# Small matmuls of attention and retention regrouped by array tile in a two-layer decoder step

## The chip, the core and the metric

The kernel runs on one core of a Trainium2 chip. The metric is device time in microseconds. Tensors lie in SBUF (128 partitions); TensorE multiplies a stationary operand (up to 128 rows by 128 columns, loaded first) with a moving one and adds into PSUM; VectorE (DVE), ScalarE (ACT) and GpSimd (POOL) do the rest, and SyncE (SP) issues most DMAs.

## The reference, cut to what matters

One inference step of a two-layer decoder: a prompt of 256 tokens and a sample group of 8 sequences with 8 new tokens each. Each layer projects x (2048 wide) to 13824 columns and runs three branches: A retention (4 heads), B pooling, C sliding-window attention (16 query heads on 4 key heads of 64). The parts that the change touches:

```python
def step(s, inp):                          # retention, one chunk
    qc, kc, vc = inp
    sc = jnp.einsum('bihd,bjhd->bhij', qc, kc) * dmask
    o = jnp.einsum('bhij,bjhv->bihv', sc, vc) + jnp.einsum('bihd,bhdv->bihv', qc, s) * q_decay
...
s = jnp.einsum('bnqkgd,bnskd->bnkgqs', qb, kb).astype(jnp.float32) * (HD_C ** -0.5)   # attention
...
s = jnp.where(valid[None, :, None, None], s + bias, jnp.finfo(jnp.float32).min)
m = jnp.maximum(jnp.max(s, -1, keepdims=True), sink)
p = jnp.exp(s - m)
p = p / (jnp.sum(p, -1, keepdims=True) + jnp.exp(sink - m))
o = jnp.einsum('bnkgqs,bnskd->bnqkgd', p.astype(vb.dtype), vb)
```

All inputs and results are fp32. A sample token attends to the last 128 cached keys of its sequence and to the new keys of that sequence up to itself; the prompt has no cache, so its first block of 128 queries sees only its own 128 keys and the second sees 256.

## The kernel before, in words

All 320 token columns (256 of the prompt, 64 of the samples) are the moving operand of the dense matmuls; the weights are stationary, in blocks of 128x128. Weights come in 596 chunks of 8 blocks. Each block is split into a high and a low fp32r part (`split_h` on ScalarE, `split_l` on VectorE, two chunks ahead; the load itself is issued six chunks ahead by SP into four buffers), and x likewise, so that each block makes three dense matmuls of 320 columns: h by xh, l by xh, h by xl (`block`, `block_low`). They fill PSUM tiles named `d`.

The small work is written as generators and put on lanes: `att` for attention, `ret0` and `ret1` for retention, and a list `misc`. After each chunk (24 dense matmuls) `pump` takes one step of each lane, unless the estimated backlog of ScalarE or VectorE is over a bound. A step's matmuls so stand in one block between two dense ones, in the order in which the steps are written; TensorE takes its instructions in that order. Small matmuls write PSUM tiles `p`, of which there are five, used in turn (`self.pp`); a new one waits until the one five allocations back has been read.

An fp32 matmul appears in the trace as two records (its weights in two parts); a transpose and an fp32r matmul as one. Where operands lie on 64 or 32 partitions, or the output on 64 or 32 partitions, a matmul uses only that part of the array's rows or columns: 64*128 means 64 rows and 128 columns.

`attention` runs once for each layer and pair of key heads (four times); `halves` are the two key heads' 64 partitions. Its items follow each other by one step each, with the stages score, first (bias and maximum), exponentials, scale, transpose:

- `block0(hf)`: scores of the first 128 prompt queries for one half, four fp32 matmuls on the 64 rows of this half; two items, two blocks. `values0` follows.
- `block1(hf, g)`: scores of the second 128 queries for two query heads, with 256 keys. q is split into high (on its half's rows) and low (on the other half's rows) in `qx`; `kx[:, hf]` holds the high part of k on both halves, `kx[r, 2]` the low part on the 64 rows of its half. Each head needs a matmul over 128 rows and a second over 64. The eight query heads of the pair make four items.
- `sample(c)`: four sequences at a time, two items. `make` multiplies with the new keys (64*128, 96 columns of `kT`), and for each sequence and half with the cache (`ck`, 64*32, 128 columns). `turned` transposes the weights; `values` has the cached values `cv` stationary and the weights moving, 32 columns for a sequence, half by half.

`retention` runs for each head and layer (eight times). In its fourth step it computes, for each c of 2, the sample outputs `po`: one full matmul (`c`, `smr`) and four that add the state's part on 32 output columns each (`a2` stationary, `s0` moving, 256 columns).

`block0`, `block1`, `sample` and the retention step are at lines 843 to 950 and 585 to 605; `mm`, `add_mm` and `tr` (L197, L201, L206) are the helpers under whose lines the matmuls stand in the profile, and `copy` (L176), `tt` (L183), `stt` (L187) those of ScalarE and VectorE.

Of the kernel before, what the change touches and what calls it, by code (L numbers as in the profile page):

```python
# [11 lines left out]
F32 = mybir.dt.float32  # L12
# [14 lines left out]
EXT = POOL_BUF + NP  # L27
HW = POOL_BUF + NT
EXTW = EXT + NB * HW
BUCKET_START = list(range(17)) + [19, 21, 24, 27, 31, 35, 40, 46, 52, 59, 67, 77, 87, 99, 113]  # L30
NEG = -3.0e38
ALPHA = (2.0 * DEPTH) ** 0.25
# [69 lines left out]
class Step:  # L102
# [197 lines left out]
    def setup(self):  # L300
        nc, io = self.nc, self.io
        self.ident = self.const("ident", [128, 128])
        make_identity(nc, self.ident[:])
        self.ident_r = self.cp.tile([128, 128], F32R, tag="ident_r", name="ident_r")
        nc.vector.tensor_copy(out=self.ident_r, in_=self.ident)
        self.ones = self.const("ones", [128, 128])
        nc.vector.memset(self.ones, 1.0)
        self.ones_r = self.cp.tile([128, 128], F32R, tag="ones_r", name="ones_r")
        nc.vector.memset(self.ones_r[:].bitcast(F32), 1.0)
        yield  # L310
        self.rot = self.const("rot", [128, 2, T], io["c_rot"], nc.sync)
# [12 lines left out]
        self.kdecS = self.const("kdecS", [128, HA, NT], io["c_kdecs"])  # L324
        self.cnt = self.const("cnt", [128, 4, 16], io["c_cnt"])
        self.pscale = self.const("pscale", [128, DEPTH, 8], io["pool_scale"])
        self.lng = self.const("lng", [128, DEPTH, 16], io["ln_g"])
        self.lnb = self.const("lnb", [128, DEPTH, 16], io["ln_b"])
        self.bmask = self.const("bmask", [128, 4, 80], io["c_bmask"])
        self.flip = self.const("flip", [128, 2], io["c_flip"])  # L330
        yield
        self.biasS = self.const("biasS", [128, 4, 160], io["bias_s"])


    def run(self):
# [210 lines left out]
    def retention(self, l, h, r):  # L546
# [48 lines left out]
        pS = self.p([128, 256])  # L595
        self.mm(pS, ktok[:, 0, :], vtok[:, 0, :])
        self.copy(s1, pS)
        for c in range(2):
            po = self.p([128, 256])
            self.mm(po, smr[:, c, :], vsT[:, c, :])  # L600
            for b in range(4):
                lo = (4 * c + b) * 32
                self.add_mm(po[32 * b:32 * b + 32, :], a2[:, 1, lo:lo + 32], s0[b // 2][:, b % 2, c, :])
# [123 lines left out]
    def done_kc(self, p, ps):  # L727
# [47 lines left out]
    def attention(self, l, p, a):  # L775
# [33 lines left out]
        self.copy(vn, pv[0:32, 2:4, :])  # L809
# [5 lines left out]
        kx = self.g([128, 3, 256], F32R, name="kx")  # L815
        pt0 = self.g([128, 2, 4, 128], name="pt0")
        for hf, r in enumerate(halves):
            self.copy(kx[r, hf, :], kT[r, 0:256])
# [8 lines left out]
        pt1 = []  # L827

        def soft(make, out):

# [3 lines left out]
                box["ps"] = make()  # L834

            def first():
                s, n, sink, nsink = out[0](box.pop("ps"))
                box["s"] = s
                box["f"] = self.softmax(s, n, sink, nsink)

# [1 line left out]

        def block0(hf):

            r = halves[hf]
# [7 lines left out]
            def biased(ps):  # L853
                s = self.m([128, 4, 128], name="sc")
                self.stt(s, ps, 0.125, bias[hf][:, :, 128:256], ALU.mult, ALU.add)
                return (s, 4, *sinks(hf, 0, 4))

            def turned(s):
# [12 lines left out]

        def block1(hf, g):

            r = halves[hf]
# [32 lines left out]

        def sample(c):

            sT = {}  # L910

            def make():
                ps = [self.p([128, 256]) for _ in range(2)]
                for hf, r in enumerate(halves):
                    self.mm(ps[hf][:, 160:256], qsf[r, c, :], kT[r, 192 + 32 * c:288 + 32 * c])
                for b in range(4):
                    o = slice(32 * b, 32 * b + 32)
                    for hf, r in enumerate(halves):
                        self.mm(ps[hf][o, 0:128], qsf[r, c, o], ck[r, 4 * c + b, :])
                return ps  # L920

            def biased(ps):
                s = self.m([128, 2, 160], name="sc")
                for hf in range(2):
                    bs = self.biasS[:, 2 * p + hf, :]
                    self.stt(s[:, hf, 0:128], ps[hf][:, 0:128], 0.125, bs[:, 0:128], ALU.mult, ALU.add)
                    self.stt(s[:, hf, 128:160], ps[hf][:, 224:256], 0.125, bs[:, 128:160], ALU.mult, ALU.add)
                ks = slice(2 * p, 2 * p + 2)
                return s, 2, self.sinkS[:, l, ks], self.nsinkS[:, l, ks]

            def turned(s):
                pt = self.p([128, 4, 128])
                for hf in range(2):
                    self.tr(pt[:, hf, :], s[:, hf, 0:128])
                    self.tr(pt[0:32, 2 + hf, :], s[:, hf, 128:160])
                t = sT[0] = self.m([128, 4, 128], name="sT")
                self.copy(t[:, 0:2, :], pt[:, 0:2, :])
                self.copy(t[0:32, 2:4, :], pt[0:32, 2:4, :])
# [11 lines left out]
            return soft(make, (biased, turned)) + [values]  # L950
# [204 lines left out]
def constants():  # L1155
# [24 lines left out]
    c = dict(c_bmask=bmask, c_flip=flip, c_rot=rot, c_dmask=dmask, c_qdec=qdec, c_kdec=kdec, c_kdecs=kdecs, c_masks=masks, c_cnt=cnt)  # L1180
    return {k: np.ascontiguousarray(v, dtype=f) for k, v in c.items()}


def bias_tables(rel):
# [6 lines left out]

    q, k = np.arange(128), np.arange(256)
    bp = table(128 + q[:, None] - k[None, :]).reshape(128, 256, 4, 4)
    b4, g, t = np.arange(128) // 32, np.arange(128) % 32 // 8, np.arange(128) % 8
    c = np.arange(160)
    new = t[:, None] - (c[None, :] - 128) % 8
    own = (c[None, :] - 128) // 8 == b4[:, None]
    dist = np.where(c[None, :] < 128, 128 + t[:, None] - c[None, :], np.where(own, new, -1))
    bs = table(dist).reshape(128, 160, 4, 4)[np.arange(128), :, :, g]
    return dict(bias_p=bp.transpose(2, 0, 3, 1), bias_s=bs.transpose(0, 2, 1))  # L1200


# [91 lines left out]
```

## Time and profile before

| | |
|---|---|
| median of 3 runs | 2295.2 us |
| lowest and highest run | 2294.62, 4468.45 us |
| profiled execution: its own time | 2294.67 us |
| profiled execution: span | 2292.8 us |
| mean granted TensorE clock | 0.995 of full speed |
| TensorE / VectorE / ScalarE / GpSimd busy | 99% / 53% / 41% / 4% |
| DMA, mean over the span | 155 GB/s |

The highest run stands apart from the other two by a factor of two; the median and the profiled execution agree with the lowest. The span is what the profiler saw between the first and the last instruction; 1.9 us of the execution lie outside it. The page gives each engine's busy time first, then the span in 40 slices, then groups of instructions with their count, their total and mean time and the idle time in front of them. Matmuls are pipelined: their recorded durations overlap, so the distance between starts, as the timeline shows it, is what one of them costs.

### The profile page before, as it was taken

How to read it: one execution, taken by the hardware profiler on the slowest of the kernel's cores; microseconds unless marked ns; L12 is line 12 of the kernel's file. 1: busy time of each engine (PE TensorE's matmuls, PEld its weight loads, DVE VectorE, ACT ScalarE, POOL GpSimd, SP SyncE). 2: the span in 40 equal slices, each digit the busy share in tenths (PEclk: the TensorE clock that was granted, in tenths of full speed). 3: DMA queues.
4: the chain of work that ended last, by engine and by line, in shares of the span. 5: the costliest groups of instructions: out<-in, count | busy, mean ns of one | idle time of the engine just before them, and what ended most of it. 6: DMA issues, size and time to landing. Idle time of an engine off the chain costs nothing.

```text
span 2292.8 us, 37711 instructions
## 1 busy us (share of the span) xinstructions
PE 2265.2 (99%) x15660; PEld 2213.3 (97%) x15660; DVE 1207.3 (53%) x1861; ACT 944.2 (41%) x1534; POOL 99.4 (4%) x155
## 2 busy tenths in 40 slices
PE   8999999999999999999999999999999999999997
PEld 8998999999999999999998989999999999999997
DVE  4645557545444444446656455575544444454566
ACT  4545445343333343333365444443434333433333
POOL 1000000000000000000020001000000000000001
PEclk9999999999999999999999999999999999999998
DMA  7443454544444444444453435445444444444442
GB/s 271 143 148 122 151 203 150 193 147 155 148 152 151 147 148 154 150 148 149 137 193 118 138 129 188 159 162 197 148 147 152 152 148 147 156 148 147 147 149 100
DMA packets 97628, 354.92 MB, mean 155 GB/s; under 512 B 11520, under 2 KB 11968, under 8 KB 97392
## 3 DMA queue, kind: packets, MB, share of 16 engines
q1 hardware_dynamic: 93312, 335.87, 43.8%
q0 software_dynamic: 4144, 16.64, 2.0%
q8 instruction: 123, 2.02, 0.4%
q14 instruction: 49, 0.40, 0.1%
HBM read 338.51 MB, written 17.88 MB: 155 GB/s over the span
## 4 chain that ended last, share of the span: by engine, by line
PE 97%; DVE 1%; ACT 1%; DMA 1%; SPq 0%; issue 0%
PE d L197 91%; PE p L197 5%; PE p L206 1%; PE p L201 1%; DMA w<-w 1%; DVE z L183 0%; ACT acc L176 0%; DVE l L183 0%; ACT h L176 0%; ACT L176 0%; SPq L340 0%; DVE z L194 0%; ACT z L176 0%; SPq L150 0%; DVE pp L187 0%
## 5 line engine op out<-in xcount | busy, mean ns | idle before, releaser
L183 DVE TENSOR_TENSOR l<-w,h 128x1024 fp32r<-128x1024 f32 (+1 forms) x597 | 737.8, 1237 | 719.9 <-ACT h L176 719.2
L197 PE MATMUL d<-xh,h 128*128 128x320 f32 x3424 | 1071.6, 313 | 7.7 <-ACT xh L176 7.6
L197 PE MATMUL d<-xh,l 128*128 128x320 f32 x3424 | 1059.2, 310 | 1.4 <-DVE l L183 1.4
L197 PE MATMUL d<-xl,h 128*128 128x320 f32 x3424 | 1049.1, 310 | 0.0
L176 ACT ACTIVATE h<-w 128x1024 fp32r<-128x1024 f32 (+1 forms) x597 | 628.3, 1053 | 517.9 <-PE d L197 351.3
L197 PEld LDWEIGHTS d<-xh,h 128*128 128x128 f32 x3424 | 644.3, 188 | 19.8 <-ACT xh L176 8.3
L197 PEld LDWEIGHTS d<-xh,l 128*128 128x128 f32 x3424 | 644.6, 188 | 2.3 <-DVE l L183 1.9
L197 PEld LDWEIGHTS d<-xl,h 128*128 128x128 f32 x3424 | 641.5, 188 | 0.0
L197 PE MATMUL d<-mgh,h 128*128 128x320 f32 x512 | 158.7, 310 | 0.0
L197 PE MATMUL d<-mgh,l 128*128 128x320 f32 x512 | 158.2, 309 | 0.0
L197 PE MATMUL d<-mgl,h 128*128 128x320 f32 x512 | 158.2, 309 | 0.0
L197 PEld LDWEIGHTS d<-mgh,h 128*128 128x128 f32 x512 | 96.1, 188 | 0.2
L197 PEld LDWEIGHTS d<-mgh,l 128*128 128x128 f32 x512 | 96.1, 188 | 0.2
L197 PEld LDWEIGHTS d<-mgl,h 128*128 128x128 f32 x512 | 96.1, 188 | 0.0
L176 ACT ACTIVATE sig<-d 128x320 f32<-128x320 f32 x64 | 28.0, 438 | 149.7 <-PE d L197 149.7
L197 PE MATMUL d<-gbh,h 128*128 128x320 f32 x256 | 79.1, 309 | 0.0
L197 PE MATMUL d<-gbh,l 128*128 128x320 f32 x256 | 79.1, 309 | 0.0
L197 PE MATMUL d<-gbl,h 128*128 128x320 f32 x256 | 79.1, 309 | 0.0
L197 PE MATMUL d<-gah,h 128*128 128x320 f32 x256 | 79.1, 309 | 0.0
L197 PE MATMUL d<-gah,l 128*128 128x320 f32 x256 | 79.1, 309 | 0.0
L197 PE MATMUL d<-gal,h 128*128 128x320 f32 x256 | 79.1, 309 | 0.0
L197 PE MATMUL d<-gch,h 128*128 128x320 f32 x256 | 79.1, 309 | 0.0
(235 smaller groups left out, 1941.3 us busy)
## 6 DMA issues: line engine op xcount, KB each, us to landing
w<-w SPq DMA_DIRECT2D x595, 512.0 KB, 3.3
s<-s SPq DMA_DIRECT2D x16, 512.0 KB, 5.8
o_rets<-s POOLq DMA_DIRECT2D x16, 512.0 KB, 5.3
bias<-bias_p SPq DMA_DIRECT2D x8, 512.0 KB, 5.5
o_x<-z SPq DMA_DIRECT2D x8, 320.0 KB, 2.2
ck<-ck SPq DMA_DIRECT2D x4, 512.0 KB, 5.2
cv<-cv SPq DMA_DIRECT2D x4, 512.0 KB, 6.5
xin<-x SPq DMA_DIRECT2D x3, 640.0 KB, 12.5
```

What stands on the lines that cost most here:

```text
L176: self.nc.scalar.activation(out=out, in_=in_, func=func, **kw)
L183: (eng or self.nc.vector).tensor_tensor(out=out, in0=a, in1=b, op=op)
L197: self.nc.tensor.matmul(out, lhsT=lhsT, rhs=rhs, start=start, stop=stop)
L201: self.nc.tensor.matmul(out, lhsT=lhsT, rhs=rhs, start=False, stop=True, skip_group_check=True)
L206: self.nc.tensor.transpose(out, in_, ident[:n, :n])
```

## The change

- **Full key rows** (`block1`): `kx` gets the low part of k on both halves, for each half separately (2 by 2 by 256 columns instead of 3 by 256). The second matmul of each head runs over all 128 rows with the same `qx` as the first.
- **Block 0's scores on two row tiles** (`block0`): the first of the two items issues all eight matmuls, the two halves in turn, into two PSUM tiles; the second item issues none.
- **Appended new keys** (`sample`): the 8 new keys of each sequence are copied behind its 128 cached ones (`ck` gets 136 columns); the scores of cache and new keys are one matmul for each sequence and half. The bias table has 136 columns. `spread_new` multiplies the weights of the new keys with a mask (`own`), so that a row has its weights only in its own sequence's 8 columns of 32.
- **Moving sample values** (`sample`): the weights are stationary and the values move. The new values come first as one full-array matmul for each half (`vn` has its 32 rows at partitions 96 to 128 under 96 rows of zeros), then the cached ones, 32 output partitions for a sequence. The output has tokens on partitions; a new stage `place` transposes it one step later. Transposes of the new part are 128 columns wide instead of 32.
- **Retention**: both full matmuls are issued before both groups of adding ones.

```diff
-        self.biasS = self.const("biasS", [128, 4, 160], io["bias_s"])
+        self.biasS = self.const("biasS", [128, 4, NK], io["bias_s"])
+        self.own = self.const("own", [128, 4, NT], io["c_own"])
...
-        for c in range(2):
-            po = self.p([128, 256])
+        pos = [self.p([128, 256]) for _ in range(2)]
+        for c, po in enumerate(pos):
             self.mm(po, smr[:, c, :], vsT[:, c, :])
+        for c, po in enumerate(pos):
             for b in range(4):
...
-        ck = self.g([128, NB, 128], name="ck")
-        nc.sync.dma_start(out=ck, in_=self.io["ck"][l, p])
+        ck = self.g([128, NB, NK], name="ck")
+        nc.sync.dma_start(out=ck[:, :, 0:128], in_=self.io["ck"][l, p])
+        self.copy(ck[:, :, 128:NK], kv[:, 0, NP:T].rearrange("p (b t) -> p b t", t=NT))
...
-        vn = vt[0:32, 256:512].rearrange("p (c v) -> p c v", c=2)
+        vn = vt[:, 256:512].rearrange("p (c v) -> p c v", c=2)
+        nc.gpsimd.memset(vn[0:96], 0.0)
...
-            self.tr(pv[0:32, 2 + c, :], vT[:, NP + 32 * c:NP + 32 * c + 32])
+            self.tr(pv[:, 2 + c, :], vT[:, NP + 32 * c - 96:NP + 32 * c + 32])
...
-            self.copy(kx[o, hf, :], kT[r, 0:256])
+            self.copy(kx[o, hf, 0], kT[r, 0:256])
             self.tt(qx[o, hf], q[r, :, 128:256], qx[r, hf].bitcast(F32), ALU.subtract)
-            self.tt(kx[r, 2, :], kT[r, 0:256], kx[r, hf, :].bitcast(F32), ALU.subtract)
+            for half in (r, o):
+                self.tt(kx[half, hf, 1], kT[r, 0:256], kx[r, hf, 0].bitcast(F32), ALU.subtract)
...
             def make():
-                ps = self.p([128, 4, 128])
+                if ps0:
+                    return
+                ps0.extend(self.p([128, 4, 128]) for _ in range(2))
                 for g in range(4):
-                    self.mm(ps[:, g, :], q[r, g, 0:128], kT[r, 0:128])
-                return ps
+                    for i, r in enumerate(halves):
+                        self.mm(ps0[i][:, g, :], q[r, g, 0:128], kT[r, 0:128])
...
-                    self.mm(ps[:, i, :], qx[:, hf, g + i, :], kx[:, hf, :], True, False)
-                    self.mm(ps[:, i, :], qx[r, hf, g + i, :], kx[r, 2, :], False, True)
+                    for part in range(2):
+                        self.mm(ps[:, i, :], qx[:, hf, g + i, :], kx[:, hf, part], part == 0, part == 1)
...
-                ps = [self.p([128, 256]) for _ in range(2)]
-                for hf, r in enumerate(halves):
-                    self.mm(ps[hf][:, 160:256], qsf[r, c, :], kT[r, 192 + 32 * c:288 + 32 * c])
+                ps = [self.p([128, NK]) for _ in range(2)]
                 for b in range(4):
                     o = slice(32 * b, 32 * b + 32)
                     for hf, r in enumerate(halves):
-                        self.mm(ps[hf][o, 0:128], qsf[r, c, o], ck[r, 4 * c + b, :])
+                        self.mm(ps[hf][o], qsf[r, c, o], ck[r, 4 * c + b, :])
...
             def values():
-                t = sT[0]
-                po = self.p([128, 4, 4, NT])
-                for hf, r in enumerate(halves):
-                    self.mm(po[r], vn[:, c, r], t[0:32, 2 + hf, :])
-                    for b in range(4):
-                        self.add_mm(po[r, b], cv[:, 4 * c + b, r], t[:, hf, 32 * b:32 * b + 32])
+                t = box.pop("t")
+                po = [self.p([128, 64]) for _ in range(2)]
+                for hf, r in enumerate(halves):
+                    self.mm(po[hf], t[:, 2 + hf, :], vn[:, c, r])
+                for b in range(4):
+                    o = slice(32 * b, 32 * b + 32)
+                    for hf, r in enumerate(halves):
+                        self.add_mm(po[hf][o], t[:, hf, o], cv[:, 4 * c + b, r])
+                box["o"] = o = self.n([128, 128], name="oT")
+                for hf in range(2):
+                    self.copy(o[:, 64 * hf:64 * hf + 64], po[hf])
+
+            def place():
+                po = self.p([128, 4, 4, NT])
+                self.tr(po.rearrange("p b g t -> p (b g t)"), box.pop("o"))
                 cols = oC[:, :, NP + 32 * c:NP + 32 * c + 32].rearrange("p g (b t) -> p b g t", t=NT)
                 self.copy(cols, po)
```

How the matmuls stand on TensorE, at three places in layer 0. First block 0's scores in the first attention (`kv` is k, `qC` is q; `d` rows are dense matmuls), before:

```order
L197 MATMUL d_680<-xl12_332,h_634 128x320
L197 MATMUL p_748<-kv_449,qC_458 128x128 x4
L197 MATMUL d_755<-xh0_110,h_678 128x320
...
L197 MATMUL d_755<-xl4_149,h_678 128x320
L197 MATMUL p_794<-kv_449,qC_458 128x128 x4
L197 MATMUL d_755<-xh8_237,h_715 128x320
```

and now, on TensorE at the same place:

```order
L198 MATMUL d_685<-xl12_332,h_638 128x320
L198 MATMUL p_755<-kv_451,qC_461 128x128
L198 MATMUL p_756<-kv_451,qC_461 128x128
L198 MATMUL p_755<-kv_451,qC_461 128x128
L198 MATMUL p_756<-kv_451,qC_461 128x128
L198 MATMUL p_755<-kv_451,qC_461 128x128
L198 MATMUL p_756<-kv_451,qC_461 128x128
L198 MATMUL p_755<-kv_451,qC_461 128x128
L198 MATMUL p_756<-kv_451,qC_461 128x128
L198 MATMUL d_767<-xh0_110,h_683 128x320
```

The second block has moved into the first, and the two PSUM tiles alternate. Second the sample values on TensorE, before, for the second group of sequences (`sT` the transposed weights, `vtok` the tile that holds `vn`):

```order
L197 MATMUL d_1407<-xl4_149,h_1305 128x320
L197 MATMUL p_1436<-sT_1402,vtok_590 64x128
L201 MATMUL p_1436<-sT_1402,cv_454 64x32 x4
L197 MATMUL p_1436<-sT_1402,vtok_590 64x128
L201 MATMUL p_1436<-sT_1402,cv_454 64x32 x4
L197 MATMUL d_1407<-xh8_237,h_1354 128x320
```

and now, with the first group's `place` (`oT`) ahead of it on TensorE:

```order
L207 MATMUL p_1407<-ident_168,oT_1366 128x128
L198 MATMUL p_1410<-vtok_593,sT_1374 128x64
L198 MATMUL p_1411<-vtok_593,sT_1374 128x64
L202 MATMUL p_1410<-cv_457,sT_1374 32x64
L202 MATMUL p_1411<-cv_457,sT_1374 32x64
L202 MATMUL p_1410<-cv_457,sT_1374 32x64
L202 MATMUL p_1411<-cv_457,sT_1374 32x64
L202 MATMUL p_1410<-cv_457,sT_1374 32x64
L202 MATMUL p_1411<-cv_457,sT_1374 32x64
L202 MATMUL p_1410<-cv_457,sT_1374 32x64
L202 MATMUL p_1411<-cv_457,sT_1374 32x64
L198 MATMUL d_1427<-xh0_110,h_1323 128x320
```

Both new-value matmuls have moved ahead of all cached ones, and the two halves alternate on each 32 output partitions. Third the retention step of the first head on TensorE, before (`c1`, `smr` the full matmul, `s00` and `s01` the state):

```order
L197 MATMUL p_2590<-bb_2373 128x256
L197 MATMUL p_2593<-c1_2161,smr_2499 128x256
L201 MATMUL p_2593<-s00_2266,a2_2049 32x256 x2
L201 MATMUL p_2593<-s01_2267,a2_2049 32x256 x2
L197 MATMUL p_2600<-c1_2161,smr_2499 128x256
L201 MATMUL p_2600<-s00_2266,a2_2049 32x256 x2
L201 MATMUL p_2600<-s01_2267,a2_2049 32x256 x2
```

and now, on TensorE:

```order
L198 MATMUL p_2608<-bb_2420 128x256
L198 MATMUL p_2611<-c1_2194,smr_2517 128x256
L198 MATMUL p_2612<-c1_2194,smr_2517 128x256
L202 MATMUL p_2611<-s00_2287,a2_2096 32x256 x2
L202 MATMUL p_2611<-s01_2288,a2_2096 32x256 x2
L202 MATMUL p_2612<-s00_2287,a2_2096 32x256 x2
L202 MATMUL p_2612<-s01_2288,a2_2096 32x256 x2
```

The second full matmul has moved ahead of the first group.

## Rows read from the trace of the kernel before

**Rows 1.** The page: busy us of each engine; TensorE's granted clock in 40 slices.
```profile
PE 2265.2 (99%) x15660; PEld 2213.3 (97%) x15660; DVE 1207.3 (53%) x1861; ACT 944.2 (41%) x1534; POOL 99.4 (4%) x155
...
PEclk9999999999999999999999999999999999999998
```

**Rows 2.** Waits of TensorE, longest: who waited for whom, us, times, longest.
```profile
PE d L197 <- ACT xh L176: 7.6, 3, 4.5
```

**Rows 3.** The page's groups, the weight split: busy, mean ns, idle before, releaser.
```profile
L176 ACT ACTIVATE h<-w 128x1024 fp32r<-128x1024 f32 (+1 forms) x597 | 628.3, 1053 | 517.9 <-PE d L197 351.3
```

**Rows 4.** Timeline of TensorE, dense matmuls, then sample scores: start, duration, instruction, count.
```profile
101.42 0.31 PE L197 MATMUL d<-xl,h 128*128 128x320 f32 x1
...
104.49 0.31 PE L197 MATMUL d<-xl,h 128*128 128x320 f32 x1
104.64 0.60 PE L206 MATMUL p<-ident,sc 128*128 128x128 f32 x4
105.17 0.47 PE L197 MATMUL p<-kv,qS 64*128 64x96 f32 x4
105.56 0.45 PE L197 MATMUL p<-ck,qS 64*32 64x128 f32 x16
105.94 0.41 PE L197 MATMUL d<-xh,h 128*128 128x320 f32 x1
```

**Rows 5.** Timeline of TensorE around one half's scores of block 0.
```profile
68.87 0.31 PE L197 MATMUL d<-xl,h 128*128 128x320 f32 x1
69.11 1.16 PE L197 MATMUL p<-kv,qC 64*128 64x128 f32 x8
70.20 0.41 PE L197 MATMUL d<-xh,h 128*128 128x320 f32 x1
70.45 0.30 PE L197 MATMUL d<-xh,l 128*128 128x320 f32 x1
```

**Rows 6.** Timeline of TensorE around one block of block 1's scores.
```profile
78.47 0.31 PE L197 MATMUL d<-xl,h 128*128 128x320 f32 x1
78.61 1.21 PE L197 MATMUL p<-kx,qx 128*128 128x256 f32 x4
...
80.01 0.31 PE L197 MATMUL d<-xh,l 128*128 128x320 f32 x1
```

**Rows 7.** Timeline of TensorE around one group's sample values.
```profile
132.82 0.31 PE L197 MATMUL d<-xl,h 128*128 128x320 f32 x1
133.06 0.43 PE L197 MATMUL p<-sT,vtok 32*64 32x128 f32 x2
133.42 0.65 PE L201 MATMUL p<-sT,cv 128*64 128x32 f32 x8
134.00 0.43 PE L197 MATMUL p<-sT,vtok 32*64 32x128 f32 x2
...
134.94 0.42 PE L197 MATMUL d<-xh,h 128*128 128x320 f32 x1
135.19 0.31 PE L197 MATMUL d<-xh,l 128*128 128x320 f32 x1
```

**Rows 8.** Timeline of TensorE, retention's sample outputs of the first head.
```profile
239.00 0.47 PE L197 MATMUL p<-c,smr 128*128 128x256 f32 x1
239.39 0.64 PE L201 MATMUL p<-s,a 128*32 128x256 f32 x8
239.96 0.39 PE L197 MATMUL p<-c,smr 128*128 128x256 f32 x1
...
240.85 0.41 PE L197 MATMUL d<-xh,h 128*128 128x320 f32 x1
```

**Rows 9.** Busy us of each engine, 68 to 136: length; PE, PEld, DVE, ACT, POOL.
```profile
68.00:136.00 68.00, 68.00 (x484) 60.44 (x483) 37.70 (x90) 32.42 (x87) 2.23 (x6) 1.00 0.36 118
```

**Rows 10.** The page's DMA issues: count, KB each, median us to landing.
```profile
ck<-ck SPq DMA_DIRECT2D x4, 512.0 KB, 5.2
```

More of the change, by code (lines that the diff above doesn't have):

```diff
@@ L29 @@
 EXTW = EXT + NB * HW
+NK = 128 + NT
 BUCKET_START = list(range(17)) + [19, 21, 24, 27, 31, 35, 40, 46, 52, 59, 67, 77, 87, 99, 113]
@@ L806, in attention @@
             self.tr(pv[:, c, :], vT[:, 128 * c:128 * c + 128])
-            self.tr(pv[0:32, 2 + c, :], vT[:, NP + 32 * c:NP + 32 * c + 32])
+            self.tr(pv[:, 2 + c, :], vT[:, NP + 32 * c - 96:NP + 32 * c + 32])
         self.copy(vtok, pv[:, 0:2, :])
-        self.copy(vn, pv[0:32, 2:4, :])
+        self.copy(vn[96:128], pv[96:128, 2:4, :])
         self.oC[p] = oC = self.g([128, 4, T], name="oC")
@@ L814, in attention @@
         qx = self.g([128, 2, 4, 128], F32R, name="qx")
-        kx = self.g([128, 3, 256], F32R, name="kx")
+        kx = self.g([128, 2, 2, 256], F32R, name="kx")
         pt0 = self.g([128, 2, 4, 128], name="pt0")
         for hf, r in enumerate(halves):
-            self.copy(kx[r, hf, :], kT[r, 0:256])
+            self.copy(kx[r, hf, 0], kT[r, 0:256])
             self.copy(qx[r, hf], q[r, :, 128:256])
@@ L822, in attention @@
             o = halves[1 - hf]
-            self.copy(kx[o, hf, :], kT[r, 0:256])
+            self.copy(kx[o, hf, 0], kT[r, 0:256])
             self.tt(qx[o, hf], q[r, :, 128:256], qx[r, hf].bitcast(F32), ALU.subtract)
-            self.tt(kx[r, 2, :], kT[r, 0:256], kx[r, hf, :].bitcast(F32), ALU.subtract)
+            for half in (r, o):
+                self.tt(kx[half, hf, 1], kT[r, 0:256], kx[r, hf, 0].bitcast(F32), ALU.subtract)
         yield
-        pt1 = []
+        pt1, ps0 = [], []
         def soft(make, out):
@@ L836, in first @@
             def first():
-                s, n, sink, nsink = out[0](box.pop("ps"))
+                s, n, sink, nsink = out[0](box.pop("ps", None))
                 box["s"] = s
@@ L843, in block0, with biased @@
         def block0(hf):
-            r = halves[hf]
             def make():
-                ps = self.p([128, 4, 128])
+                if ps0:
+                    return
+                ps0.extend(self.p([128, 4, 128]) for _ in range(2))
                 for g in range(4):
-                    self.mm(ps[:, g, :], q[r, g, 0:128], kT[r, 0:128])
-                return ps
-            def biased(ps):
+                    for i, r in enumerate(halves):
+                        self.mm(ps0[i][:, g, :], q[r, g, 0:128], kT[r, 0:128])
+            def biased(_):
                 s = self.m([128, 4, 128], name="sc")
-                self.stt(s, ps, 0.125, bias[hf][:, :, 128:256], ALU.mult, ALU.add)
+                self.stt(s, ps0[hf], 0.125, bias[hf][:, :, 128:256], ALU.mult, ALU.add)
                 return (s, 4, *sinks(hf, 0, 4))
@@ L872, in block1 @@
         def block1(hf, g):
-            r = halves[hf]
             def make():
@@ L908, in sample @@
         def sample(c):
-            sT = {}
+            box = {}
             def make():
-                ps = [self.p([128, 256]) for _ in range(2)]
-                for hf, r in enumerate(halves):
-                    self.mm(ps[hf][:, 160:256], qsf[r, c, :], kT[r, 192 + 32 * c:288 + 32 * c])
+                ps = [self.p([128, NK]) for _ in range(2)]
                 for b in range(4):
@@ L918, in make, with spread_new, turned @@
                     for hf, r in enumerate(halves):
-                        self.mm(ps[hf][o, 0:128], qsf[r, c, o], ck[r, 4 * c + b, :])
+                        self.mm(ps[hf][o], qsf[r, c, o], ck[r, 4 * c + b, :])
                 return ps
             def biased(ps):
-                s = self.m([128, 2, 160], name="sc")
+                box["s"] = s = self.m([128, 2, NK + 32], name="sc")
                 for hf in range(2):
-                    bs = self.biasS[:, 2 * p + hf, :]
-                    self.stt(s[:, hf, 0:128], ps[hf][:, 0:128], 0.125, bs[:, 0:128], ALU.mult, ALU.add)
-                    self.stt(s[:, hf, 128:160], ps[hf][:, 224:256], 0.125, bs[:, 128:160], ALU.mult, ALU.add)
+                    self.stt(s[:, hf, 0:NK], ps[hf], 0.125, self.biasS[:, 2 * p + hf, :], ALU.mult, ALU.add)
                 ks = slice(2 * p, 2 * p + 2)
-                return s, 2, self.sinkS[:, l, ks], self.nsinkS[:, l, ks]
-            def turned(s):
+                return s[:, :, 0:NK], 2, self.sinkS[:, l, ks], self.nsinkS[:, l, ks]
+            def spread_new():
+                s = box["s"]
+                self.tt(
+                    s[:, :, NK:].rearrange("p h (b t) -> p h b t", t=NT),
+                    s[:, :, 128:NK].unsqueeze(2).to_broadcast([128, 2, 4, NT]),
+                    self.own.unsqueeze(1).to_broadcast([128, 2, 4, NT]), ALU.mult,
+                )
+            def turned(_):
+                s = box.pop("s")
                 pt = self.p([128, 4, 128])
@@ L934, in turned @@
                     self.tr(pt[:, hf, :], s[:, hf, 0:128])
[L935 to L938, printed above, removed]
+                    self.tr(pt[:, 2 + hf, :], s[:, hf, NK - 96:])
+                t = box["t"] = self.m([128, 4, 128], name="sT")
+                self.copy(t, pt)
             def values():
-                t = sT[0]
+                t = box.pop("t")
[10 more added lines that the diff above has]
+            def place():
                 po = self.p([128, 4, 4, NT])
-                for hf, r in enumerate(halves):
-                    self.mm(po[r], vn[:, c, r], t[0:32, 2 + hf, :])
-                    for b in range(4):
-                        self.add_mm(po[r, b], cv[:, 4 * c + b, r], t[:, hf, 32 * b:32 * b + 32])
+                self.tr(po.rearrange("p b g t -> p (b g t)"), box.pop("o"))
                 cols = oC[:, :, NP + 32 * c:NP + 32 * c + 32].rearrange("p g (b t) -> p b g t", t=NT)
                 self.copy(cols, po)
-            return soft(make, (biased, turned)) + [values]
+            stages = soft(make, (biased, turned))
+            scale = stages[3]
+            stages[3] = lambda: (scale(), spread_new())
+            return stages + [values, place]
         items = [block0(0), block0(1) + [values0]]
@@ L1179, in constants @@
     flip = -np.stack([r % 32 == 1, jg == 1], axis=1).astype(f)
-    c = dict(c_bmask=bmask, c_flip=flip, c_rot=rot, c_dmask=dmask, c_qdec=qdec, c_kdec=kdec, c_kdecs=kdecs, c_masks=masks, c_cnt=cnt)
+    own = np.broadcast_to((jb[:, None] == np.arange(4))[:, :, None], (128, 4, NT))
+    c = dict(c_own=own, c_bmask=bmask, c_flip=flip, c_rot=rot, c_dmask=dmask, c_qdec=qdec, c_kdec=kdec, c_kdecs=kdecs, c_masks=masks, c_cnt=cnt)
     return {k: np.ascontiguousarray(v, dtype=f) for k, v in c.items()}
@@ L1193, in bias_tables @@
     bp = table(128 + q[:, None] - k[None, :]).reshape(128, 256, 4, 4)
[L1194 to L1199, printed above, removed]
+    g, t = np.arange(128) % 32 // 8, np.arange(128) % 8
+    dist = 128 + t[:, None] - np.arange(NK)[None, :]
+    bs = table(dist).reshape(128, NK, 4, 4)[np.arange(128), :, :, g]
     return dict(bias_p=bp.transpose(2, 0, 3, 1), bias_s=bs.transpose(0, 2, 1))
```

## The prediction

> **What bounds the kernel.** I read the page first, then the waits of TensorE, then the timeline of TensorE around each kind of small matmul. TensorE is busy for 2265.2 of 2292.8 us [rows 1], and its granted clock stays at the upper of its two levels, 2.4 GHz, in all slices but the last [rows 1]. It hardly waits for anyone: its longest entry in the waits is 7.6 us in three waits [rows 2]. ScalarE, which prepares the weights, waits for TensorE instead: 351.3 us of its idle time before the split ended with a dense matmul [rows 3]. So a nanosecond taken out of TensorE's stream is a nanosecond off the end, as long as nothing new makes it wait.
>
> Busy time says nothing about where TensorE loses time, since matmuls overlap. The distance between starts does. In a dense stretch 22 matmuls start from 101.42 to 104.49: 21 steps of 0.146 us for 320 columns [rows 4]. A block of small matmuls therefore costs the time from the last dense start before it to the second dense start behind it, less two steps (0.29).
>
> The same rows price a **turnaround**, when the next matmul uses another part of the array (64*128, 128*32 and so on are rows*columns in use). Between full-array matmuls the step is 0.146; before block 0's scores it is 0.24 (68.87 to 69.11), 0.09 more. Behind them the first dense matmul starts at 70.20 and the second at 70.45, 0.25 instead of 0.146: its weights were not loaded ahead, 0.10 more [rows 5]. Inside, eight records (two for each fp32 matmul) take 1.09 us including one uncovered load and one drain, so 0.111 each for 128 columns.
>
> **The change, part by part.** There are four attentions (2 layers, 2 pairs of key heads) and eight retention heads.
>
> *Block 0's scores on two row tiles.* Before, two blocks of 1.58 - 0.29 = 1.29 us [rows 5]. Now the two halves alternate in one block, each on its own 64 rows and in its own PSUM tile. That two row tiles overlap is seen in the sample scores: four records on two row tiles take 0.39, an uncovered load, 2 x 0.08 of streaming and a drain, which leaves no room for four streams in a row [rows 4]. I take full overlap: one block of 1.30, a gain of 1.28 x 4 = 5.1 us. Without any overlap the second half adds 8 x 0.111 = 0.89, and 0.39 x 4 = 1.6 us is left, from the turnaround.
>
> *Full key rows in block 1.* Four matmuls alternate between 128 and 64 rows, and every change is a turnaround: 80.01 - 78.47 - 0.29 = 1.25 us [rows 6]. With 128 rows throughout, nothing turns around. A full-array fp32r matmul with 256 columns should take 256/320 of the dense step, 0.118: four are 0.47. Gain 0.78; four such blocks in each attention, 16 in all, 12.5 us. Ends: at 0.111 (the 128-column load, rows 5) 13.0; at the dense step of 0.146, 10.7. I take 0.118, since these are of the dense matmul's type. Half of them stand behind four transposes, which do not change.
>
> *Appended new keys.* The group with the new keys disappears: from 105.17 to 105.56, 0.39 [rows 4]. The cache matmuls get 136 columns instead of 128, two records on each tile, 0.01 more. The turnaround in front of them was there already. 0.38 x 8 = 3.0 us, with little doubt. The sample's four transposes before the values keep their number and width.
>
> *Moving sample values.* Before: 135.19 - 132.82 - 0.29 = 2.08 us for one sample group, four small groups on 32*64 and 128*64 with a turnaround between each [rows 7]. Now: four full-array records, bound by the 128-column load, 4 x 0.11 = 0.44; a turnaround 0.04 (a 64-column stream is shorter than its load); then 16 records on four column tiles, four deep on each. For this the cache scores are the model: 16 records on eight tiles, two deep, take 0.38 [rows 4], which is a short load 0.03, two streams of 0.107, 0.05 between the first and last tile, and a drain. Four streams of 64 columns, 0.055 each, make 0.39. Then 0.10 of uncovered load. Sum 0.97. The added transpose at the end is 0.11: four of them and a drain take 0.53 [rows 4]. 2.08 - 1.08 = 1.00, eight times: 8.0 us. If the column tiles do not overlap, 16 records at 0.058 (eight in 0.58 up to the next group, rows 7) add 0.66, and 2.7 us is left.
> The Trainium skill's page "TensorE: Matmul & The Clock Gate" (section "Wait — 56ns, not 53.3ns?") says that starts of matmuls come no closer than about 25 ns however small they are. By that the 16 records would take 0.13 longer and the time would be 2264.4. The trace says otherwise: 16 records in 0.38, of which 0.107 is the last stream and 0.09 the drain, start at most 12 ns apart [rows 4].
>
> *Retention.* Before, from 239.00 to 240.85: matmul 0.39, group 0.57, matmul and group 0.89 [rows 8]. With both full matmuls first, the first loses its drain (0.30), the second takes 0.118 + 0.09, and the joint group has four streams on each column tile instead of two: 0.57 + 2 x 0.215 = 1.00. That is 1.51 against 1.85, 0.34 for each head, 2.7 us; at least 0.31, one turnaround out (0.09 + 0.03 for a 32-column load) and back (0.09 + 0.10). Two PSUM tiles are now held at once.
>
> *Other engines.* Two more half-height subtractions for the keys, one more product for the spread of the new weights, two copies of 64 columns instead of one wide copy, fewer bias additions, one memset on POOL. I cost them at nothing: in the first attention VectorE works 37.7 and ScalarE 32.4 of 68 us [rows 9], and weights are split two chunks ahead. Should this cover go, one late split costs up to 1.05 us [rows 3]. The key-cache load writes 512-byte pieces instead of whole rows. It lands after 5.2 us [rows 10] and is issued many steps before the sample scores use it, so that twice that would not be seen. The weight loads behind it on SP's queue run up to six chunks ahead.
>
> **Sum:** 5.1 + 12.5 + 3.0 + 8.0 + 2.7 = 31.3 us off the profiled execution's 2294.67 (0.5 below the median of the runs shown): **2263.4 us**, 1.4% less. With all lower ends, 1.6 + 10.7 + 3.0 + 2.7 + 2.5 = 20.5: 2274.2. With the upper ones 31.8: 2262.9, and some us less if waits happen to shorten.
>
> **Rivals.**
> *The tiles do not overlap.* Row tiles in block 0 and column tiles in the values run one after the other. Then about 2274, still from turnarounds. Against it: the two-tile and eight-tile groups of rows 4. For it: no group before is four deep on one tile except with 128*64. Chance 0.10.
> *Slower: TensorE waits for PSUM.* The five PSUM tiles for small work now serve two tiles at once in block 0 and in retention, and three instead of one for a sample's values. If a step's matmuls have to wait until ScalarE has read an older tile, and its copy stands behind a weight split, one step loses 1.05 us [rows 3]. Some 13 steps in each of four attentions make 55 us: 2263 + 55 = 2318. It decides from 0.6 us a step on (31.3/52). The page "TensorEngine Tiling (Array Packing)" of the Trainium skill (section "PSUM Bottleneck") warns of just this: tiling speeds up TensorE, not the evacuation of PSUM. The trace is against it here: no wait of this kind [rows 2], both reading engines about half idle [rows 9], and a step comes once in 24 dense matmuls, 3.5 us, with most tiles freed a step earlier. Chance 0.04.
> *No change.* The time saved is spent waiting for weights, 2294. Against it: ScalarE waits for TensorE before the split [rows 3]. Chance 0.03.
>
> **How the numbers follow.** The forecast has 0.80, the three rivals 0.17, things not listed 0.03. The range runs from 2258 (upper ends and a few us of other waits that move) to 2274 (no overlap). A difference of 2%, 46 us, is about what a measurement of this kernel can tell from no change; 31 us lies within it. Faster by over 2% (under 2249) needs half as much again as every upper end: 0.04. Slower by over 2% needs PSUM waits of more than 1.4 us a step: 0.02. Within 2%: 0.94.
>
> **What would show it.** In the timeline after: one block for block 0 with 16 records in about 1.1 us; four 128*128 records with 256 columns 0.12 apart and a next dense start without an extra 0.10; no group of new keys; the values as two groups with about 0.97 us; two smr matmuls in a row. Block 0 taking two us, or values near 1.6, would show that tiles run in turn. Entries of several us "PE p <- ACT" in the waits of TensorE would make the forecast wrong.

## The result

The changed kernel takes 2263.43 us (median of 4 runs, 2263.24 to 2264.09) against 2295.23 before; the ratio is 0.9864, 95% interval 0.9852 to 0.9875. The profiled execution takes 2263.36 us with a span of 2261.6, so 31.2 us of span are gone. Of the runs shown of before, 4468.45 lies apart and is not part of the ratio.

TensorE's busy time on the page fell by 31.7 us; that of the other engines rose by 1.6 to 2.7:

```profile
PE 2233.5 (99%) x15636; PEld 2198.4 (97%) x15636; DVE 1209.9 (53%) x1861; ACT 946.9 (42%) x1546; POOL 101.0 (4%) x160
```

The waits of TensorE after (who waited for whom, us in all, times, longest) have the entry of [rows 2], a little longer, and nothing new; no small matmul waits for a copy on ScalarE:

```profile
PE d L198 <- ACT xh L177: 8.3, 4, 4.7
PE p L198 <- DVE S L184: 2.2, 2, 1.1
PE d L198 <- DVE l L184: 1.7, 4, 0.7
PE p L198 <- DVE s L188: 0.6, 2, 0.3
PE p L198 <- DVE sp_r L184: 0.5, 2, 0.2
```

The timeline of TensorE after, at the places of [rows 5 to 8] and the sample scores of [rows 4] (start, duration, instruction, count), in this order: block 0's scores, a block of block 1's, the second group's sample scores, its values with the first group's `place` ahead, and retention:

```profile
68.20 0.31 PE L198 MATMUL d<-xl,h 128*128 128x320 f32 x1
68.44 1.16 PE L198 MATMUL p<-kv,qC 64*128 64x128 f32 x16
...
69.79 0.30 PE L198 MATMUL d<-xh,l 128*128 128x320 f32 x1
...
76.53 0.31 PE L198 MATMUL d<-xl,h 128*128 128x320 f32 x1
76.67 0.64 PE L198 MATMUL p<-kx,qx 128*128 128x256 f32 x4
77.15 0.31 PE L198 MATMUL d<-xh,h 128*128 128x320 f32 x1
77.30 0.31 PE L198 MATMUL d<-xh,l 128*128 128x320 f32 x1
...
99.24 0.60 PE L207 MATMUL p<-ident,sc 128*128 128x128 f32 x4
99.77 0.46 PE L198 MATMUL p<-ck,qS 64*32 64x136 f32 x16
100.16 0.41 PE L198 MATMUL d<-xh,h 128*128 128x320 f32 x1
...
122.41 0.31 PE L198 MATMUL d<-xl,h 128*128 128x320 f32 x1
122.56 0.27 PE L207 MATMUL p<-ident,oT 128*128 128x128 f32 x1
122.67 0.56 PE L198 MATMUL p<-vtok,sT 128*128 128x64 f32 x4
123.15 0.45 PE L202 MATMUL p<-cv,sT 128*32 128x64 f32 x16
123.53 0.41 PE L198 MATMUL d<-xh,h 128*128 128x320 f32 x1
123.78 0.31 PE L198 MATMUL d<-xh,l 128*128 128x320 f32 x1
...
224.13 0.58 PE L198 MATMUL p<-c,smr 128*128 128x256 f32 x2
224.65 1.07 PE L202 MATMUL p<-s,a 128*32 128x256 f32 x16
225.65 0.42 PE L198 MATMUL d<-xh,h 128*128 128x320 f32 x1
```

What to see: 16 records of block 0 take the 1.16 us that eight took before. Behind block 1's four matmuls the first dense step is 0.15 (77.15 to 77.30), not 0.25: no turnaround is left. The cache scores follow the transposes directly. The values are two groups, and the two smr matmuls stand in a row. Each block's price by the rule of the prediction (last dense start before to second dense start behind, less 0.29):

| | before | forecast | after | number |
|---|---|---|---|---|
| block 0's scores | 2 x 1.29 | 1.30 | 1.59 - 0.29 = 1.30 | 4 |
| block 1's scores | 1.25 | 0.47 | 0.77 - 0.29 = 0.48 | 16 |
| new keys' scores | 0.39 | 0.01 | 0.01 (their neighbours have 0.53 and 0.39, before 0.53 and 0.38) | 8 |
| sample values and place | 2.08 | 1.08 | 1.37 - 0.29 = 1.08 | 8 |
| retention, first smr to dense | 1.85 | 1.51 | 1.52 | 8 |

Summed over all their blocks in the two traces, the five parts give 5.1 + 12.3 + 3.1 + 8.0 + 2.7 = 31.2 us, the whole fall of the span.

### The profile page after: what moved, and what is told of

It is laid out like the page before. It is cut to its first block, busy times and chain, and to the rows that moved or that the text cites. A ratio compares the mean times of both kernels' runs of the same rounds, so it can differ in the third digit from the quotient of the medians.

```text
span 2261.6 us, 37677 instructions
## 1 busy us (share of the span) xinstructions
PE 2233.5 (99%) x15636; PEld 2198.4 (97%) x15636; DVE 1209.9 (53%) x1861; ACT 946.9 (42%) x1546; POOL 101.0 (4%) x160
## 4 chain that ended last, share of the span: by engine, by line
PE 97%; DVE 1%; ACT 1%; DMA 0%; issue 0%; SPq 0%; ACTq 0%
PE d L198 91%; PE p L198 4%; PE p L207 1%; DMA w<-w 0%; DVE z L184 0%; PE p L202 0%; DVE l L184 0%; ACT acc L177 0%; ACT z L177 0%; ACT h L177 0%; ACT L177 0%; ACT xh L177 0%; DVE xl L184 0%; SPq L342 0%; DVE z L195 0%
## 6 DMA issues: line engine op xcount, KB each, us to landing
xin<-x SPq DMA_DIRECT2D x3, 640.0 KB, 12.5
```

## The experiments

Times are medians of the runs of each kernel, and ratios are to runs of the kernel before on the same chip, whose medians are 2294.2 to 2294.8. Differences are taken to the 2263.43 of the changed kernel, which stood beside 2295.23; so a single difference is uncertain by up to about 1 us. Repeated runs of one kernel spread by 0.5 to 2.6 us.

**Each part undone.** Block 1 first:

```diff
...
-                    for part in range(2):
-                        self.mm(ps[:, i, :], qx[:, hf, g + i, :], kx[:, hf, part], part == 0, part == 1)
+                    self.mm(ps[:, i, :], qx[:, hf, g + i, :], kx[:, hf, :], True, False)
+                    self.mm(ps[:, i, :], qx[halves[hf], hf, g + i, :], kx[halves[hf], 2, :], False, True)
```

> The changed kernel with block 1's scores as before (low part of k on 64 rows, matmuls alternating 128 and 64 rows). Theory T, that every change between parts of the array costs a turnaround and nothing else matters: each of 16 blocks goes from 0.48 back to 1.25 us, so 2263.4 + 16 x 0.78 = 2275.8 us. Rival, that the gain came from shifted steps or other engines and not from this block: within 2 us of 2263.4.

Measured: 2275.7 us, ratio to before 0.9918 (0.9903 to 0.9933). 12.3 us came back for this block alone.

Block 0 in two items again:

```diff
-                if ps0:
-                    return
-                ps0.extend(self.p([128, 4, 128]) for _ in range(2))
+                ps0.append(self.p([128, 4, 128]))
                 for g in range(4):
-                    for i, r in enumerate(halves):
-                        self.mm(ps0[i][:, g, :], q[r, g, 0:128], kT[r, 0:128])
+                    self.mm(ps0[hf][:, g, :], q[halves[hf], g, 0:128], kT[halves[hf], 0:128])
```

> The changed kernel with block 0's scores in two blocks again, one for each half. Theory T: one more block of 1.28 us in each of four attentions, 2263.4 + 5.1 = 2268.5. Rival, that the two row tiles did not overlap and only a turnaround was saved: 2263.4 + 4 x 0.39 = 2265.0.

Measured: 2268.69 us, 0.9888 (0.9872 to 0.9905): 5.3 us, the value for full overlap.

Sample values as before (`turned` and `values` as they stood, no `place`):

> The changed kernel with the sample values as before: values stationary, 32 weight columns moving, half by half, no transposes at the end. Theory T: each of eight groups goes from 0.94 + 0.11 back to 2.08 us, 2263.4 + 8 x 1.03 = 2271.6. Rival, that the column tiles hardly overlap and the added transposes eat what is left: 2263.4 to 2266.

Measured: 2270.82 us, 0.9897 (0.9882 to 0.9911): 7.4 us.

New keys in a group of their own (`make`, `biased` and the bias table as they stood, no `spread_new`):

> The changed kernel with the new keys' scores as a matmul group of their own (64*128, 96 columns) ahead of the cached ones again, and 160 columns of softmax. Theory T: eight groups of 0.39 us come back, 2263.4 + 3.1 = 2266.5. Rival, that they were hidden: 2263.4.

Measured: 2266.47 us, 0.9877 (0.9861 to 0.9894): 3.0 us.

Retention by turns:

```diff
-        pos = [self.p([128, 256]) for _ in range(2)]
-        for c, po in enumerate(pos):
-            self.mm(po, smr[:, c, :], vsT[:, c, :])
-        for c, po in enumerate(pos):
+        for c in range(2):
+            po = self.p([128, 256])
+            self.mm(po, smr[:, c, :], vsT[:, c, :])
```

> The changed kernel with retention's full matmul and adding group by turns again. Theory T: one turnaround out and back for each of eight heads, 2263.4 + 8 x 0.33 = 2266.0. Rival, that four-deep column tiles run no better than two separate groups: 2263.4.

Measured: 2266.29 us, 0.9875 (0.9861 to 0.989): 2.9 us.

Together 12.3 + 5.3 + 7.4 + 3.0 + 2.9 = 30.9 of the 31.8 us between the medians. Within the uncertainty of five such differences the parts add up, and with the 31.2 us of the blocks in the traces no gain is left that shifted steps or other engines would have to explain.

**Turnaround or narrow matmul?** The same 64-row matmuls as before, but behind both full ones:

```diff
...
                 for i in range(2):
-                    for part in range(2):
-                        self.mm(ps[:, i, :], qx[:, hf, g + i, :], kx[:, hf, part], part == 0, part == 1)
+                    self.mm(ps[:, i, :], qx[:, hf, g + i, :], kx[:, hf, :])
+                for i in range(2):
+                    self.add_mm(ps[:, i, :], qx[halves[hf], hf, g + i, :], kx[halves[hf], 2, :])
```

> As the previous kernel, but in each block the two 128-row matmuls stand first and the two 64-row ones behind them: the same matmuls, one excursion instead of two. Theory T: 0.118 + 0.21 + 0.10 + 0.118 + 0.21 + 0.10 = 0.86 us a block, so 2263.4 + 16 x 0.38 = 2269.5. Rival, that a 64-row matmul is slow in itself: no better than with the matmuls alternating, 2275.8. Rival, that the second matmul waits for its low part of k: also 2275.8.

In this order the first head's low part is no longer added to its high part; number, size and place of the matmuls are those meant. Measured: 2268.97 us, 0.9891 (0.9876 to 0.9906), 5.5 us over the changed kernel and 6.7 under the alternating order. The timeline of TensorE in this kernel:

```profile
76.46 0.31 PE L198 MATMUL d<-xl,h 128*128 128x320 f32 x1
76.61 0.40 PE L198 MATMUL p<-kx,qx 128*128 128x256 f32 x2
76.94 0.50 PE L202 MATMUL p<-kx,qx 64*128 64x256 f32 x2
...
77.62 0.31 PE L198 MATMUL d<-xh,l 128*128 128x320 f32 x1
```

77.62 - 76.46 - 0.29 = 0.87 us, against 1.25 alternating [rows 6] and 0.48 on full rows. The same four matmuls cost 0.38 less with one excursion instead of two, and one excursion costs 0.39 over none. So 64 rows are not slow in themselves; the changes between parts of the array are what was paid. Nor is it the number format: the plain fp32 matmuls on the full array (`vtok`, `sT`) start 0.15 behind a dense fp32r one, like another dense one (121.07 to 121.22 in the last timeline of this section).

**How far do tiles run ahead?** Block 0 with all of one half first:

```diff
-                for g in range(4):
-                    for i, r in enumerate(halves):
+                for i, r in enumerate(halves):
+                    for g in range(4):
                         self.mm(ps0[i][:, g, :], q[r, g, 0:128], kT[r, 0:128])
```

> The changed kernel with block 0's eight matmuls in one block, but all four of one half ahead of all four of the other. Theory A, that TensorE hands matmuls on to each row tile at least four ahead, so that the tiles overlap in any order: one block stays at 1.28 us and the time at 2263.4. Theory B, that tiles overlap only as far as their matmuls alternate: the second half follows the first, 0.89 us more a block, 2263.4 + 3.6 = 2267.0; a look-ahead of two would give about half of it.

Measured: 2265.37 us, 0.9874 (0.9859 to 0.9889), between both theories. The timeline of TensorE:

```profile
68.35 0.31 PE L198 MATMUL d<-xl,h 128*128 128x320 f32 x1
68.58 1.71 PE L198 MATMUL p<-kv,qC 64*128 64x128 f32 x16
...
70.47 0.31 PE L198 MATMUL d<-xh,l 128*128 128x320 f32 x1
```

2.12 - 0.29 = 1.83 us, 0.53 over the alternating order and 0.36 under what no overlap would give. The two halves overlap in part. Record by record, the fifth of the first half starts at 69.134 and the first of the second half at 69.140: it sets out ahead of the three of the first half that stand before it in the program and are still to start. Both theories fell. Two by two:

```diff
-                for g in range(4):
+                for g0 in (0, 2):
                     for i, r in enumerate(halves):
-                        self.mm(ps0[i][:, g, :], q[r, g, 0:128], kT[r, 0:128])
+                        for g in (g0, g0 + 1):
+                            self.mm(ps0[i][:, g, :], q[r, g, 0:128], kT[r, 0:128])
```

> The changed kernel with block 0's matmuls two by two: two of one half, two of the other, and again. Four by four, the second tile started 0.555 us after the first, when four of the first tile's eight records were left or running. Theory C, that about four records (two fp32 matmuls) of one tile can be ahead of another tile's first: two by two overlaps fully, block of 1.28 us, 2263.4. Theory B, that only alternating matmuls overlap: the second tile starts two to three records late in each round, about 0.2 to 0.3 us a block, 2264.5.

Measured: 2263.28 us, 0.9866 (0.985 to 0.9883). The timeline of TensorE:

```profile
68.08 0.31 PE L198 MATMUL d<-xl,h 128*128 128x320 f32 x1
68.32 1.26 PE L198 MATMUL p<-kv,qC 64*128 64x128 f32 x16
...
69.76 0.31 PE L198 MATMUL d<-xh,l 128*128 128x320 f32 x1
```

1.68 - 0.29 = 1.39: nearly the full overlap, 0.1 short of it. Theory C holds but for this 0.1, which is too small for the run times to show (4 x 0.1 = 0.4 us). Record by record it lies in the second round, where a record of the second half is followed by its next after 0.21 instead of 0.11: one weight load that was not covered. The first records of the two halves start 0.014 apart, again with three records of the first half still to start. So two fp32 matmuls (four records) of one tile may stand ahead of the other tile's, not four; three were not tried. The values of the change have just that: the two halves' two matmuls on each column tile, then the next tile. Their sixteen records start in rounds of four, the first four 0.013 apart, as if one on each tile, although twelve records stand ahead of the fourth tile's first; so the limit seems to hold for each tile by itself.

**Are PSUM tiles short?** The pool with four instead of five:

```diff
-        self.pp = pool("psp", 5, space=bass.MemoryType.PSUM)
+        self.pp = pool("psp", 4, space=bass.MemoryType.PSUM)
```

> The changed kernel with four PSUM tiles for the small work instead of five. If five tiles leave slack (the forecast): no step holds more than four new tiles, and the time stays within 1.5 us of 2263.4. If tiles are already short, as the slower rival of the prediction had it: 0.6 to 1.05 us in many of some 50 steps, 2285 or more, and entries of TensorE waiting for ScalarE in the small matmuls.

Measured: 2266.42 us, 0.9877 (0.9862 to 0.9892), 3.0 us slower: neither. The timeline of TensorE at the second group's sample scores (in brackets idle time and releaser):

```profile
98.65 0.60 PE L207 MATMUL p<-ident,sc 128*128 128x128 f32 x4
99.18 0.42 PE L198 MATMUL p<-ck,qS 64*32 64x136 f32 x2
99.86 0.46 PE L198 MATMUL p<-ck,qS 64*32 64x136 f32 x14 [0.27 <-DVE sc L188]
100.25 0.41 PE L198 MATMUL d<-xh,h 128*128 128x320 f32 x1
```

and that of VectorE in the same kernel, the bias additions for the first group:

```profile
99.52 0.50 DVE L188 SCALAR_TENSOR_TENSOR sc<-p,biasS 128x136 f32<-128x136 f32 x2
```

The second half's tile is the one that still holds the first group's scores, which VectorE reads from 99.52 on. From the first of these scores to the next dense start it is 100.25 - 99.18 = 1.07 us, against 0.39 in the changed kernel (99.77 to 100.16): 0.68 of delay, of which the profile counts 0.27 as idle. It comes in each of the four attentions (in one of them 0.20 of it already at the first group's scores): 2.7 of the 3.0 us. With five tiles the step has the one tile more that it needs. A wait for a PSUM tile, as the slower rival had it, was so one tile away; but it is for VectorE's bias addition and not for ScalarE behind a weight split, and it comes at one step of each attention, not at each of some fifty.

**A step further.** Retention's state updates of all eight sequences in one step and one block, on four row tiles, instead of two steps with two row tiles each:

```diff
-        for b in range(4):
-            rr = slice(32 * b, 32 * b + 32)
-            pu = self.p([128, 2, 256])
-            for c in range(2):
+        pus = [self.p([128, 2, 256]) for _ in range(4)]
+        for c in range(2):
+            for b, pu in enumerate(pus):
+                rr = slice(32 * b, 32 * b + 32)
                 self.mm(pu[:, c, :], ksT[rr, c, :], vsT[rr, c, :])
+        for b, pu in enumerate(pus):
...
-                yield
+        yield
```

> A step further by the same theory: in the changed kernel the retention state updates (32*128, two sequences to a row tile) are two blocks of 0.64 us for each of eight heads, each with two row tiles and a turnaround. Here all four row tiles go in one block, into four PSUM tiles. Theory T: one block of 0.65 instead of 1.27, 8 x 0.62 = 5.0 us less: 2258.4. Rival, that four row tiles do not stream at once or that four PSUM tiles held together make TensorE wait: 2263 or more.

Measured: 2258.55 us, 0.9843 (0.9829 to 0.9856), 4.9 us less than the change. The timeline of TensorE in the changed kernel, around two row tiles:

```profile
234.42 0.31 PE L198 MATMUL d<-xl,h 128*128 128x320 f32 x1
234.66 0.51 PE L198 MATMUL p<-c 32*128 32x256 f32 x4
...
235.34 0.31 PE L198 MATMUL d<-xh,l 128*128 128x320 f32 x1
```

and in this one, around four:

```profile
235.22 0.31 PE L198 MATMUL d<-xl,h 128*128 128x320 f32 x1
235.46 0.51 PE L198 MATMUL p<-c 32*128 32x256 f32 x8
...
236.15 0.30 PE L198 MATMUL d<-xh,l 128*128 128x320 f32 x1
```

Eight records on four row tiles take the 0.51 us that four took on two.

Then the two sample groups in step:

```diff
+        at = [0, 1, 2, 3, 4, 5, 7, 7]
         for t in range(len(items) + 6):
-            for i, stages in enumerate(items):
+            for i, stages in zip(at, items):
```

> The previous kernel, and the two groups of sample sequences take their steps together, so that their scores stand side by side in one block, and their values too. Theory T: in each attention one turnaround out and back less for the scores (0.31 and some overlap of the drain) and about 0.2 for the values: 4 x 0.5 = 2.0 us less, 2256.4. Rival, that five PSUM tiles are too few for four score tiles at once: TensorE waits for ScalarE or VectorE, 2258 or more.

Measured: 2257.57 us, 0.9839 (0.9825 to 0.9852), half of the forecast gain; its runs (2257.3 to 2257.8) lie below those of the kernel before this step (2258.1 to 2259.1). No wait for a score tile appears in TensorE's list. The values of both groups, timeline of TensorE:

```profile
121.07 0.31 PE L198 MATMUL d<-xl,h 128*128 128x320 f32 x1
121.22 0.55 PE L198 MATMUL p<-vtok,sT 128*128 128x64 f32 x4
121.70 0.45 PE L202 MATMUL p<-cv,sT 128*32 128x64 f32 x16
122.08 0.66 PE L198 MATMUL p<-vtok,sT 128*128 128x64 f32 x4
122.67 0.45 PE L202 MATMUL p<-cv,sT 128*32 128x64 f32 x16
...
123.30 0.31 PE L198 MATMUL d<-xh,l 128*128 128x320 f32 x1
```

123.30 - 121.07 - 0.29 = 1.94, as much as two groups of 0.97 apart: between them TensorE goes back to the full array, and that return costs the same whether dense matmuls or the next group's full ones follow. The 0.2 forecast for the values was wrong for that reason. With the scores alone in step, and the second group held back one step:

```diff
+        items[7].insert(1, lambda: None)
+        at = [0, 1, 2, 3, 4, 5, 7, 7]
-        for t in range(len(items) + 6):
+        for t in range(len(items) + 7):
```

> The kernel with joint state updates, and of the two sample groups the scores alone taken together; the second group then idles one step, so that values and transposes stand apart as in the changed kernel. Taken together in all steps, the scores cost 2.86 us instead of 3.20 for an attention, but values and transposes 0.09 more. If that split is right: 4 x 0.34 = 1.4 us under 2258.5, 2257.2. If the later order matters more: 2258.5 or above.

Measured: 2258.84 us, 0.9846 (0.9832 to 0.9861): no gain over 2258.55. The scores did cost 2.86 us for an attention, but the waits of TensorE have a new row, transposes waiting for VectorE's scaling:

```profile
PE p L207 <- DVE sc L193: 1.0, 2, 0.7
```

By the rule of the blocks the two transposes that wait cost 0.97 and 0.57 us more than others like them, 1.5 in all, as much as the 1.4 that the scores were to give. The joint state updates are what is worth keeping, 4.9 us; taking the two groups together in all steps adds 1.0.

## Why the prediction was right, step by step

- **That TensorE's stream sets the end** was right: 31.2 us of span went with 31.7 us of TensorE's busy time, and its waits, 12.8 us in all before, are 13.3 after.
- **The turnaround as the unit of account** was right, and shown apart from the narrow matmuls by the regrouped block 1: 0.38 for one excursion. But not every change of the columns in use costs one. Before, half of the transposes of `kv` had 32 columns, in turn with full ones, on TensorE:

```profile
L206 PE MATMUL p<-ident,kv 128*128 128x128 f32 x8 | 2.0, 272 | 0.0
L206 PE MATMUL p<-ident,kv 128*32 128x128 f32 x8 | 2.0, 272 | 0.0
```

Their blocks of four cost 0.44 us, and 0.44 now that all have 128 columns. The same holds for the sample's weights. There the prediction says that the four transposes keep their width, but the change widened two of the four from 32 to 128 columns; a block of them behind eight value matmuls took 2.46 us and still does, so the slip cost the sum nothing. Why these transposes pay no turnaround, no run here tells.
- **Block 0** was right in size (5.1 forecast, 5.3 when undone). The overlap that was taken from a group two deep holds since the halves alternate; it would not have held for four matmuls of one half in a row.
- **Block 1**: 0.48 instead of 0.47, 12.3 us when undone against 12.5. The guess of 256/320 of a dense step, 0.118, was nearly right: the starts are 0.117 to 0.120 apart.
- **New keys**: 3.0 and 3.0.
- **Values**: the block is 1.08, as forecast; undone it is 7.4 us against 8.0. The blocks differ by 1.00 in the traces, undone too (2.08), so the missing 0.6 us lies outside them and within the spread of the runs. By the Trainium skill's figure of about 25 ns between starts (page "TensorE: Matmul & The Clock Gate", section "Wait — 56ns, not 53.3ns?") the 16 records would, as an estimate, have taken at least 15 x 0.025 = 0.375 us from first to last start. The trace after shows 0.38 from the first start to the first dense start behind, and 0.09 of drain (by so much later a start on another part of the array comes [rows 5]) and 0.05 of the last stream lie in it: on the mean, starts are at most 0.24/15 = 16 ns apart, on four tiles.
- **Retention**: 1.52 instead of 1.51, 2.9 us against 2.7.
- **The rivals.** The tiles overlapped. What the prediction had for the rival, that no group before is four deep on one tile except with 128*64, was a misreading: the sums of squares of retention's output (`sums`, sixteen records on four column tiles) are. The timeline of TensorE in the kernel before:

```profile
376.17 0.35 PE L197 MATMUL p<-sq,ones 128*32 128x80 f32 x8
376.34 0.32 PE L201 MATMUL p<-sq,ones 128*32 128x80 f32 x8
376.59 0.41 PE L197 MATMUL d<-xh,h 128*128 128x320 f32 x1
```

From 376.17 to 376.59, the next dense start, is 0.42 us, the nearest model for the 0.38 of the values and an answer to the rival before any run. PSUM waits did not happen with five tiles, but the reason given, that tiles are freed a step earlier, was too easy: with four, 0.68 us comes at one step. The work on other engines, costed at nothing, was hidden; the key-cache load lands after 5.3 us instead of 5.2.

In the traces each part came out within 0.2 us of its forecast. That the median agrees to 0.1 us is partly luck: runs of one kernel differ by about 1 us. And 46 us was too much for what a measurement can tell from no change: the interval of the ratio, 0.9852 to 0.9875, spans 5.3 us, and differences of 3 us were told apart above.

## What to carry to other kernels

Where one stream of matmuls bounds the kernel, count changes between parts of the array before counting matmuls: here an excursion cost 0.39 us in block 1, as much as three full matmuls of 256 columns, and 0.33 in retention, and filling rows with more operand or grouping what uses the same tiles removes it. Whether a change costs one is read from the starts, not from the columns in use: narrow transposes between full ones cost nothing here. Narrow groups want alternating tiles, two fp32 matmuls deep at most, and a PSUM tile for each group that is still unread. Joining two groups paid where no other part of the array was used between them (the scores), and not where one was (the values).

## What the runs showed of the hardware that was not expected

- A tile can run about four records (two fp32 matmuls) ahead of another tile's first. With four matmuls in a row the second row tile joined five records late, 0.53 us, and with two it lost 0.1.
- Four row tiles of 32 rows take the time of two: 0.51 us for eight records and for four.
- Transposes of 32 columns between transposes of 128 cost no turnaround: 0.44 us for four, mixed or not.
